# Moving part of the second layer's modulation products from the first layer's feed-forward into the second layer's mixer

## The chip, the cores and the metric

The kernel runs on one core of one Trainium2 chip. Its time is device microseconds of one execution; the median of several executions is compared. A profile of one execution shows what each engine did: TensorE (PE, with its weight loads as PEld), VectorE (DVE), ScalarE (ACT), GpSimd (POOL) and SyncE (SP), which issues every DMA here.

## The reference, cut to what matters

One inference step of a diffusion backbone: two layers over 640 tokens (128 of a prompt, 512 latent ones) of width 1024. Each layer is a mixer (four branches, gated and merged) and a convolutional feed-forward, both wrapped in modulated norms:

```python
def _trunk_layer(x, mod, lw, ctx):
    sh_a, sc_a, g_a, sh_f, sc_f, g_f = jnp.split(mod[:, None, :], 6, axis=-1)
    h = _rmsnorm(x, lw['g_pre_mix']) * (1.0 + sc_a) + sh_a
    m, cache = _token_mixer(h, lw, ctx)
    x = x + g_a * _rmsnorm(m, lw['g_post_mix'])
    h = _rmsnorm(x, lw['g_pre_ffn']) * (1.0 + sc_f) + sh_f
    x = x + g_f * _rmsnorm(_conv_ffn(h, lw), lw['g_post_ffn'])
    return x, cache
```

The modulation `mod` is `silu(cond) @ w_mod[i] + b_mod[i]`, 6144 numbers for each of two conditions (context and latent). They depend on no token, so they can be computed at any time before they are used. In blocks of 128 the 6144 are blocks 0 to 47: 0 to 15 are the shift and scale ahead of the mixer, 16 to 47 the gate, shift, scale and gate from the mixer's end on.

## The kernel before

Activations lie with features on the partitions, eight tiles of 128 x 640 for the width of 1024. Every linear layer streams its float32 weights in tiles of 128 x 512 (256 KB): a DMA brings `wr`, ScalarE rounds it to `wh`, VectorE takes the rest `wl = wr - wh`, and TensorE adds three products (`wh` with the activation's high part `ah`, `wh` with its low part `al`, `wl` with `ah`) in halves of 320 tokens.

The modulation products of everything but the first 16 blocks of layer 0 are not on TensorE. `mod_units` makes them on VectorE, one block of 128 outputs at a time, against a silu tile that is spread over all partitions:

```python
for j in blocks:
    for hf in hv:
        w = self.sbt(512, "wm", 2)
        self.load(w[:, :512], self.A["wmod"][l, j][:, hf * 512 : hf * 512 + 512])
        for q in range(2):
            ...
            self.nc.vector.scalar_tensor_tensor(junk[:, :512], w[:, :512], 0.5, si, ALU.mult, ALU.mult, accum_out=acc)
            yield
```

So a block is 2 loads of 256 KB into one of two buffers `wm` and 4 products ("units" from here on), each one VectorE instruction that writes `wj` and one that reads the accumulator. For each half `hv` the generator first loads the two conditions (`g<-in_c`), and ScalarE and VectorE make the silu tiles `silc`, two buffers.

The generator is drained in small portions. `fill(n)` takes n units from it and ties them to the TensorE instruction that was recorded last, so that they can't start before it. `merge` calls `fill(8)` ahead of each of 8 output blocks for the first and the third branch (64 units each; the second has `fill(0)`), `merge_out` calls `fill(2)` 16 times, the feed-forward calls `fill(5)` after each of its 22 up-projection blocks and `fill(2)` ahead of each block of a down-projection, and `fill(1000)` takes what is left.

In layer 0 the mixer's fills take 128 units, the blocks 16 to 47 of layer 0 itself. Then `mixer` starts a generator for all 48 blocks of layer 1: 192 units, of which 32 go in `merge_out` and 160 in the feed-forward of layer 0. In the mixer and the feed-forward of layer 1 nothing is left to fill with.

The program's order is not the order of the code. Every operation is recorded, then `order()` plays the whole kernel with a table of costs and emits it engine by engine in the order of the starts it found. A unit has the bias `BEHIND`, a late due time, unless what reads its result is due earlier; weight loads have the bias `AHEAD`. All instructions are issued from one line of the program (L608 in every row of the profile), so rows are told apart by their tiles. Each engine then works through its own list in order, SyncE with the DMA issues too.

Of the kernel before, what the change touches and what calls it, by code (L numbers as in the profile page):

```python
# [613 lines left out]
class Net:  # L614
# [1375 lines left out]
    def mixer(self, l, x, hh, hl):  # L1990

        nc, A = self.nc, self.A
        self.hb = self.sbt(32, "hb", 1)
        self.tsc(self.hb, self.P("bmg", 0, 32), 0.5)
        self.rope_load("64")
        win = A["win"][l]
        y = self.ssd(l, hh, hl)
        zd = self.spill("zd", 4)
        self.ph("ssd.z%d" % l)
        self.gates(win, range(W_Z, W_Z + 4), zd)(hh, hl)  # L2000
        r = self.ret_in(l, hh, hl)
        o = self.ssd_end(l, y, zd)
        r = self.ret_states(l, *r)
        gd = self.spill("gd", 4)
        self.ph("ret.g%d" % l)
        self.gates(win, range(W_RG, W_RG + 4), gd)(hh, hl)
        self.flush()
        merged = [self.X(j) for j in range(8)]
        o2 = self.ret(l, *r, gd)
        self.merge(l, 0, hh, hl, o, merged, 8)  # L2010
        self.flush()
        r = self.att_in(l, hh, hl)
        o = self.spill("od", 4)
        self.att(l, *r, o)
        self.merge(l, 1, hh, hl, o2, merged, 0)
        r = self.mla_in(l, hh, hl)
        o2 = self.spill("od", 4)
        self.mla(l, *r, o2)
        self.merge(l, 2, hh, hl, o, merged, 8)
        mods = self.modraw  # L2020
        if l == 0:
            self.fill(1000)
            self.mod_new()
            self.filler = self.mod_units(1, range(48), ((0,), (1,)), self.sil_tile)
        return self.merge_out(l, x, hh, hl, o2, merged, mods)

    def merge_out(self, l, x, hh, hl, o, merged, mods):
# [73 lines left out]
    def ffn(self, l, x, Gf, hh, hl):  # L2101
        A = self.A
        self.ph("ffn%d" % l)
        self.fcs = self.sbt(88, "fcs", 1)
        o, _ = PC["fcw"]
        for t in range(3):
            self.tsc(self.fcs[:, t * 22 : (t + 1) * 22], self.pc[:, o + t * 44 + 22 : o + t * 44 + 44], 0.5)
        o2, _ = PC["fcb"]
        self.tsc(self.fcs[:, 66:88], self.pc[:, o2 + 22 : o2 + 44], 0.5)
        acc = [self.O(j) for j in range(8)]  # L2110
        pre = [self.F() for _ in range(6)]
        specs = []
        for i in range(6):
            specs.append((A["wup"][l, (22 if i % 2 else 0) + i // 2], 8, hh, hl, 128,
                          lambda p, hv, i=i: self.conv_put(pre[i], p, hv)))
        self.lins(specs)
        fh, fl = {}, {}
        self.modw = self.g

        def up(f):  # L2120
            buf = pre[2 * f + 1] if f < 3 else self.conv_lin(A["wup"][l, 22 + f], 8, hh, hl)
            gt = self.conv(buf, [self.fcs[:, t * 22 + f : t * 22 + f + 1] for t in range(3)], self.fcs[:, 66 + f : 67 + f])
            sg = self.m()
            self.silu_half(sg[:, :641], gt[:, :641], 641)
            buf = pre[2 * f] if f < 3 else self.conv_lin(A["wup"][l, f], 8, hh, hl)
            up = self.conv(buf, [self.pc[:, o + t * 44 + f : o + t * 44 + f + 1] for t in range(3)], self.pc[:, o2 + f : o2 + f + 1])
            self.tt(sg[:, :641], sg[:, :641], up[:, :641])
            fh[f], fl[f] = self.F(F32R), self.F(F32R)
            for s, d in ((slice(0, 128), slice(0, 128)), (slice(129, 641), slice(128, 640))):
                self.act(fh[f][:, d], sg[:, s])  # L2130
                self.last = self.tt(fl[f][:, d], sg[:, s], fh[f][:, d], ALU.subtract)
            self.fill(5)

        def down(f0, f1):
            for j in range(8):
                self.fill(2)
                for p, c in self.lin_fm(A["wdn"][l, j][:, f0 * 128 : f1 * 128], f1 - f0, [fh[f] for f in range(f0, f1)], [fl[f] for f in range(f0, f1)]):
                    if f0 == 0:
                        self.act(acc[j][:, c], p)
                    else:  # L2140
                        self.last = self.tt(acc[j][:, c], acc[j][:, c], p, ALU.add)

        for f in FFN_ORDER:
            if isinstance(f, tuple):
                down(*f)
            else:
                up(f)
        f0, f1 = FFN_LAST
        self.fill(1000)
        Am = S = None  # L2150
        if l + 1 < L:
            self.params(l + 1)
            S, Am = self.mod_get(0, self.modraw), self.mod_scale(1, "gpm", self.modraw)
            hh, hl = self.split_tiles()
        fh, fl = [fh[f] for f in range(f0, f1)], [fl[f] for f in range(f0, f1)]
        norm = self.halves_to_norm(8, acc, acc, x, Gf, Am, S, hh, hl, "dn%d" % l, 1.0, self.xd[l + 1] if l + 1 < L else A["oy"])
        self.lins([(A["wdn"][l, j][:, f0 * 128 : f1 * 128], f1 - f0, fh, fl, 128, norm(j)) for j in range(8)])
        for k in range(8):
            self.dump("x", x[k][:, :T], l, k)
        return hh, hl  # L2160
# [38 lines left out]
```

## Time and profile before

| | us |
|---|---|
| median of 3 executions (lowest, highest) | 2915.98 (2914.49, 2923.48) |
| the profiled execution | 2915.53 |
| its span in the trace, first to last instruction | 2913.4 |
| TensorE busy | 2849.6 (98%) |
| VectorE busy | 2151.2 (74%) |
| ScalarE busy | 1390.3 (48%) |
| DMA queue of SyncE | 326.46 MB, 35.7% of 16 engines |

The span is 2.1 us shorter than the execution's own time. Shares are means over a span in which the stages differ much, so the two layers, which do the same work one after the other, are set side by side stage by stage.

### The profile page before, as it was taken

To read this page: it belongs to the slowest core of one execution; us is meant where nothing else is said; L and a number is where in the kernel's file an instruction comes from. 1 tells how busy PE (TensorE), PEld (TensorE's weight loads), DVE (VectorE), ACT (ScalarE), POOL (GpSimd) and SP (SyncE) were. 2 spreads that over 40 slices of the span, in tenths; PEclk is the share of its full clock that TensorE was granted. 3 is DMA by queue.
4 is the path that set the end of the run, shared out by engine and by line. 5 is a ranking of instruction groups with operands and counts; after the bars stand their busy time and mean duration, and the time that the engine had idled before them with its cause. 6 is when DMAs were issued, how large, how long until landed. Compare 5 with 4: busy or idle time off the path is not lost.

```text
span 2913.4 us, 50176 instructions
## 1 busy us (share of the span) xinstructions
PE 2849.6 (98%) x18638; PEld 2683.4 (92%) x18638; DVE 2151.2 (74%) x4548; ACT 1390.3 (48%) x3013; POOL 79.0 (3%) x99
## 2 busy tenths in 40 slices
PE   8999999999999999999989999999999999999998
PEld 4889998898899999999988899989988999999997
DVE  5895748648889899888878953586597577666667
ACT  4444347557735543333455443474576465333333
POOL 0000010000000000000000000100000000000000
PEclk9999999999999999999989999999999999999999
DMA  5224531234375444444332232212433444222223
GB/s 214 66 81 144 177 97 41 63 121 128 110 221 189 156 141 152 132 133 132 108 120 74 75 132 89 79 39 67 149 107 95 141 138 131 74 76 77 76 73 112
DMA packets 193412, 329.67 MB, mean 113 GB/s; under 512 B 20880, under 2 KB 54288, under 8 KB 193168
## 3 DMA queue, kind: packets, MB, share of 16 engines
q1 hardware_dynamic: 193168, 326.46, 35.7%
q8 instruction: 147, 2.41, 0.3%
q14 instruction: 97, 0.79, 0.1%
HBM read 293.41 MB, written 32.96 MB: 112 GB/s over the span
## 4 chain that ended last, share of the span: by engine, by line
PE 86%; DVE 6%; DMA 3%; issue 2%; ACT 1%; SPq 0%; POOL 0%; DVEq 0%; POOLq 0%; ACTq 0%
PE lin L608 70%; PE st L608 11%; PE pv L608 5%; DVE m L608 2%; DVE wl L608 1%; DMA wm<-in_wmod 1%; DVE wj L608 1%; DVE X L608 1%; DMA K<-in_wmod 0%; ACT K L608 0%; DVE al L608 0%; DMA vd<-g 0%; DVE K L608 0%; ACT m L608 0%; DVE g L608 0%
## 5 line engine op out<-in xcount | busy, mean ns | idle before, releaser
L608 PE MATMUL lin<-ah,wh 128*128 128x320 f32 (+1 forms) x3776 | 1158.3, 314 | 11.7 <-ACT K L608 6.9
L608 PE MATMUL lin<-al,wh 128*128 128x320 f32 (+1 forms) x3776 | 1150.4, 312 | 7.7 <-DVE al L608 7.5
L608 ACT ACTIVATE wh<-wr 128x512 fp32r<-128x512 f32 (+2 forms) x796 | 490.2, 617 | 1049.0 <-PE lin L608 725.7
L608 PE MATMUL lin<-ah,wl 128*128 128x320 f32 x3744 | 943.6, 311 | 0.5 <-DVE wl L608 0.4
L608 DVE TENSOR_TENSOR wl<-wr,wh 128x512 fp32r<-128x512 f32 (+2 forms) x790 | 530.0, 672 | 307.2 <-ACT wh L608 297.0
L608 PEld LDWEIGHTS lin<-ah,wh 128*128 128x128 f32 (+1 forms) x3776 | 710.2, 189 | 25.1 <-issue 8.8
L608 PEld LDWEIGHTS lin<-al,wh 128*128 128x128 f32 (+1 forms) x3776 | 708.1, 188 | 19.9 <-DVE al L608 11.4
L608 PEld LDWEIGHTS lin<-ah,wl 128*128 128x128 f32 x3744 | 649.2, 188 | 8.4 <-issue 3.8
L608 PE MATMUL lin<-K,wh 128*128 128x320 f32 (+1 forms) x1472 | 293.8, 313 | 6.1 <-DVE O L608 4.3
L608 DVE TENSOR_TENSOR m<-m,m 128x512 fp32r<-128x512 f32 (+6 forms) x393 | 246.3, 632 | 51.7 <-ACT m L608 45.5
L608 ACT ACTIVATE m<-st 128x512 fp32r<-128x512 f32 (+3 forms) x480 | 220.6, 524 | 102.7 <-PE st L608 90.0
L608 DVE SCALAR_TENSOR_TENSOR wj<-wm,silc 128x512 bf16<-128x512 f32 x320 | 219.8, 687 | 37.4 <-DMA wm<-in_wmod 34.2
L608 PEld LDWEIGHTS lin<-K,wh 128*128 128x128 f32 x1472 | 237.5, 189 | 8.5 <-ACT m L608 4.5
L608 PE MATMUL lin<-O,wh 128*128 128x320 f32 x1024 | 214.6, 311 | 0.4 <-DVE O L608 0.4
L608 PE MATMUL pv<-m,K 128*128 128x512 f32 (+2 forms) x832 | 204.6, 344 | 0.9 <-ACT m L608 0.5
L608 PE MATMUL lin<-K,wl 128*128 128x320 f32 (+1 forms) x736 | 185.0, 312 | 0.9 <-DVE wl L608 0.9
L608 PEld LDWEIGHTS lin<-O,wh 128*128 128x128 f32 x1024 | 166.9, 188 | 5.0 <-DVE O L608 0.7
L608 PEld LDWEIGHTS pv<-m,K 128*64 128x64 f32 (+1 forms) x832 | 116.2, 160 | 23.9 <-issue 6.2
L608 PE MATMUL st<-Q,K 128*128 128x512 f32 (+3 forms) x480 | 133.7, 381 | 0.1
L608 PE MATMUL lin<-O,wl 128*128 128x320 f32 x512 | 132.9, 310 | 0.0
L608 PEld LDWEIGHTS lin<-K,wl 128*128 128x128 f32 x736 | 128.4, 189 | 1.6 <-DVE wl L608 1.6
L608 DVE TENSOR_REDUCE nm<-st 128x1 f32<-128x320 f32 (+1 forms) x288 | 122.7, 461 | 7.3 <-PE st L608 5.8
(195 smaller groups left out, 2957.2 us busy)
## 6 DMA issues: line engine op xcount, KB each, us to landing
wr<-in_wup SPq DMA_DIRECT2D x196, 256.0 KB, 2.7
wr<-in_wmg SPq DMA_DIRECT2D x160, 256.0 KB, 2.8
wm<-in_wmod SPq DMA_DIRECT2D x160, 256.0 KB, 3.0
wr<-in_win SPq DMA_DIRECT2D x142, 256.0 KB, 2.6
wr<-in_wdn SPq DMA_DIRECT2D x94, 256.0 KB, 2.7
wr<-in_wbr SPq DMA_DIRECT2D x80, 256.0 KB, 2.7
wr<-in_wout SPq DMA_DIRECT2D x64, 256.0 KB, 2.8
g<-od SPq DMA_DIRECT2D x32, 320.0 KB, 4.1
```

The source lines that it names most:

```text
L608: f(*[_plain(v) for v in o.args], **{k: _plain(v) for k, v in o.kw.items()})
```

## The change

The generator of layer 1 is split. Blocks 0 to 15 (64 units) stay where all 48 were: 32 units in `merge_out` of layer 0 and 32 in its feed-forward, now three after each up-projection block in place of five. Blocks 16 to 47 (128 units) get a generator of their own, which is set up at the end of layer 0's feed-forward and is drained by the fills that layer 1's mixer has already, `fill(8)` ahead of each output block of its first and third merge. The `fill(1000)` in `mixer` is now called in both layers.

```diff
         mods = self.modraw
+        self.fill(1000)
         if l == 0:
-            self.fill(1000)
             self.mod_new()
-            self.filler = self.mod_units(1, range(48), ((0,), (1,)), self.sil_tile)
+            self.filler = self.mod_units(1, range(16), ((0,), (1,)), self.sil_tile)
         return self.merge_out(l, x, hh, hl, o2, merged, mods)
...
                 self.last = self.tt(fl[f][:, d], sg[:, s], fh[f][:, d], ALU.subtract)
-            self.fill(5)
+            self.fill(3)
...
             S, Am = self.mod_get(0, self.modraw), self.mod_scale(1, "gpm", self.modraw)
             hh, hl = self.split_tiles()
+            self.filler = self.mod_units(l + 1, range(16, 48), ((0,), (1,)), self.sil_tile)
```

## Rows read from the trace of the kernel before

**Rows 1.** The page: busy time by engine, and the chain that ended last.
```profile
PE 2849.6 (98%) x18638; PEld 2683.4 (92%) x18638; DVE 2151.2 (74%) x4548; ACT 1390.3 (48%) x3013; POOL 79.0 (3%) x99
PE 86%; DVE 6%; DMA 3%; issue 2%; ACT 1%; SPq 0%; POOL 0%; DVEq 0%; POOLq 0%; ACTq 0%
```

**Rows 2.** Everything on tile `wm`: durations in ns min/median/max, first and last start.
```profile
L608 DVE SCALAR_TENSOR_TENSOR wj<-wm,silc x320: 672/685/696, 278.2 to 1390.5; 128x512 bf16<-128x512 f32 x160
L608 DVE DVE_READ_ACCUMULATOR wj<-wm,silc x320: 73/82/86, 278.8 to 1391.2; 128x1 f32 x160
L608 SPq DMA_DIRECT2D wm<-in_wmod x160: 327/328/1765, 271.1 to 1382.6; - x160
DMA to landing us min/median/max: 2.4/3.0/6.2
```

**Rows 3.** Long pieces of the whole chain: start, length, what, matmuls.
```profile
1052.28 366.03 PE lin L608 x2494
...
2486.08 366.05 PE lin L608 x2494
```

**Rows 4.** Equal stretches of both layers: length, busy times, PEclk, DMA share, GB/s.
```profile
260.15:386.47 126.32, 122.88 (x876) 120.82 (x874) 90.52 (x235) 42.01 (x110) 8.66 (x14) 1.00 0.56 174
1709.56:1831.95 122.39, 122.39 (x876) 120.82 (x874) 47.73 (x105) 40.11 (x108) 8.03 (x14) 1.00 0.34 104
795.08:916.78 121.70, 116.82 (x774) 114.65 (x772) 110.24 (x268) 54.23 (x103) 0.00 (x0) 0.99 0.70 217
2237.38:2350.06 112.68, 112.68 (x772) 112.68 (x770) 63.20 (x102) 52.54 (x99) 0.00 (x0) 1.00 0.44 135
916.78:996.30 79.52, 78.42 (x535) 76.99 (x535) 72.20 (x181) 47.63 (x100) 3.13 (x3) 1.00 0.54 170
2350.06:2430.08 80.02, 78.21 (x536) 77.27 (x537) 60.90 (x141) 47.55 (x100) 3.74 (x3) 1.00 0.45 139
1052.28:1418.31 366.03, 366.03 (x2496) 366.03 (x2497) 323.63 (x736) 126.54 (x286) 0.00 (x0) 1.00 0.43 132
2486.08:2852.13 366.05, 366.05 (x2496) 366.05 (x2497) 232.93 (x408) 123.50 (x284) 0.00 (x0) 1.00 0.25 75
```

**Rows 5.** The same stretches, VectorE's instructions on `wj` alone (two a unit).
```profile
260.15:386.47 126.32, 44.58 (x128) 1.00 0.56 174
...
795.08:916.78 121.70, 52.76 (x152) 0.99 0.70 217
...
916.78:996.30 79.52, 13.94 (x40) 1.00 0.54 170
...
1052.28:1418.31 366.03, 110.87 (x320) 1.00 0.43 132
```

**Rows 6.** TensorE's waits, first merge of layer 0: total us, times, longest.
```profile
PE st L608 <- DVE m L608: 3.4, 2, 2.3
```

**Rows 7.** TensorE's waits from the third merge to the first output half, layer 0.
```profile
PE lin L608 <- DVE al L608: 3.9, 3, 2.0
```

**Rows 8.** VectorE's waits in that stretch.
```profile
DVE wj L608 <- DMA wm<-in_wmod: 9.3, 13, 1.6
```

**Rows 9.** SyncE's waits ahead of a DMA issue in that stretch.
```profile
SPq L608 <- DVE wj L608: 28.4, 35, 1.8
```

**Rows 10.** The chain in that stretch: start, length, what.
```profile
864.31 0.70 DVE wj L608 x2
865.03 4.50 DMA wm<-in_wmod
...
892.29 0.41 DVE al L608
892.75 24.03 PE lin L608 x162
```

**Rows 11.** GpSimd's powers in the first merge, layer 0.
```profile
L608 POOL TENSOR_TENSOR rq<-rq,mhalf 128x4 f32<-128x4 f32 x5 | 5.7, 1138 | 64.1 <-DVE rq L608 64.1
```

**Rows 12.** The same in the first merge of layer 1.
```profile
L608 POOL TENSOR_TENSOR rq<-rq,mhalf 128x4 f32<-128x4 f32 x5 | 5.0, 1008 | 59.1 <-DVE rq L608 59.1
```

**Rows 13.** A pair of stretches with no unit in either layer.
```profile
618.57:795.08 176.51, 171.16 (x1036) 150.23 (x1035) 139.53 (x247) 126.81 (x270) 5.18 (x13) 1.00 0.40 128
2064.07:2237.38 173.31, 171.50 (x1036) 150.22 (x1035) 139.63 (x247) 127.08 (x270) 5.18 (x13) 1.00 0.40 127
```

## The prediction

> **What bounds the kernel now.** Start with the page: TensorE is busy for 98% of the span, VectorE for 74%, and the chain that ended last is 86% TensorE [rows 1]. So time is lost only where something makes TensorE stop, and a gain can come only from such a place. The mean does not say where the units hurt. For that the kernel carries its own control: both layers run the same mixer and the same feed-forward, layer 0 with units in its gaps and layer 1 without any. The whole chain gives pieces of TensorE work that recur in both layers with the same count; taken as boundaries, they give equal stretches whose lengths can be subtracted.
>
> First look at the feed-forward, which the change relieves. It is one unbroken piece of 2494 matmuls in each layer, 366.03 us with units and 366.05 us without [rows 3]. In the table of stretches TensorE is busy for the whole of both, although VectorE works 323.63 us in one and 232.93 us in the other [rows 4]. VectorE at 88% still never makes TensorE wait there.
>
> Then look at the mixer, which the change loads. From the first merge on, 876 matmuls take 126.32 us in layer 0, where 64 units run, and 122.39 us in layer 1: 3.93 us more. From the third merge to the norm after the first half of the output projection it is 121.70 us against 112.68 us: 9.02 us more, with TensorE never idle in layer 1. The stretch after that is 0.50 us shorter in layer 0 (79.52 against 80.02) although it holds 20 units [rows 4, 5].
>
> What the reader is to see in the waits: TensorE waits for `m` of VectorE in the first merge (3.4 us in two waits, 2.3 the longest) [rows 6] and for `al`, the low half of the activations, in the later stretch (3.9 us in three) [rows 7]. Behind both is VectorE's in-order list. There it waits for `wm` to land (9.3 us in 13 waits) [rows 8], and SyncE in turn waits 28.4 us for VectorE to give a `wm` buffer back [rows 9], with weight loads behind it in the same queue. The chain shows the loop: two products, a `wm` transfer of 4.50 us, later `al`, then TensorE [rows 10].
>
> **The change part by part.** *The count.* 48 blocks are 192 units, 16 are 64, the other 32 are 128. The merges of layer 1 call for 8 x 8 units twice, 128, so the new generator is used up in the mixer and both `fill(1000)` find at most its end. Layer 0's mixer and `merge_out` keep the units they have: the first 32 of the old and of the new generator are the same blocks and the same half. In layer 0's feed-forward 160 units become 32.
>
> *What is taken out.* 128 units leave the feed-forward of layer 0. Each is a product of 685 ns and an accumulator read of 82 ns, 0.767 us, so 98.2 us of VectorE; with them go 64 loads of 256 KB, 328 ns each on SyncE, 21.0 us of its list [rows 2]. All lay beside 366.03 us of gapless TensorE [rows 3, 4]. Gain: 0. The cover would have to be gone for it to be worth more, and the layer without any unit shows that it then takes 366.05 us. The last product ended near 1391 us [rows 2], before the stretch ends, so the norm that follows does not wait for units either. `fill(3)` only spaces the 32 units that remain; 0, for the same reason.
>
> *What is added.* The new generator loads the two conditions and makes silu tiles for each half, four sets more than before: 4 loads of 256 KB, 4 ScalarE passes and 4 VectorE passes of the units' shape, by their row some 0.69 us each. In layer 0's stretches the same sets lie inside the difference already, so they are not added again.
>
> *What is put in: the first merge of layer 1.* 64 units with 32 loads, the same instructions at the same fills as layer 0 has. Bound from below: 0, if the waits in layer 0 were chance. From above: the whole 3.93 us. VectorE's work goes from 47.73 to about 97 us of 122 (64 x 0.767 = 49.1), which is not full, yet layer 0 with 90.52 us lost 3.93 [rows 4]. I take 3.93, since it is the same code under the same load.
>
> A small share of this may come over GpSimd. Five powers on the way to the retention norm take 1138 ns each in layer 0 [rows 11] and 1008 ns in layer 1 [rows 12], 0.65 us in all. The Trainium skill, "SBUF — State Buffer", section "Who interferes with whom", has a VectorE instruction with two inputs in SBUF contend with a GpSimd instruction that reads SBUF, and a unit reads two. The rows agree in sign; by that rule alone the added time of this merge would be about 0.65 us, an estimate, against the 3.93 us of the stretches.
>
> *What is put in: the third merge of layer 1.* 64 units, 32 loads, and a new wait: `merge_out` needs gate, shift and scale from these units for the norm after the first output half. Before, they were ready long ahead. Queued behind a late unit on VectorE are `wl` of the weights, `al` of the activations and the gates' products, and TensorE waits for each of them. Price from below: 0. From above: 9.02 us. VectorE's need is 63.20 + 49.1 = 112.3 us in a stretch of 112.68 us, with waits for `wm` on top (9.3 us in layer 0), so it can't all fit. One thing is different: layer 0's stretch holds 76 units, 12 of them of the next set [rows 5]. These come last, when the 24.03 us piece of TensorE from 892.75 on is running already [rows 10], so I do not count them as a cause. I take 9.02.
>
> *What follows it.* The stretch after gave 0.50 us back in layer 0, which I take as the end of the same shift: -0.50. The norm was not late there, so I price the new wait itself at 0. The granted clock was 0.99 to 1.00 in all these stretches [rows 4], so I add nothing for it.
>
> Sum: 0 + 3.93 + 9.02 - 0.50 = 12.45 us, on the profiled execution's 2915.53: 2927.98, say 2928. The median of the runs is 2915.98, half a microsecond from that execution, so the sum holds for the median as well.
>
> **The rivals.** *Hidden (not slower).* The place is VectorE's list between layer 1's third merge and the first output half, and what decides is whether its 112.3 us of work run with under a microsecond of waits, or 9 us of units slide into later gaps. For it: VectorE is at 56% there (63.20 of 112.68), and TensorE's own waits in layer 0 are just 3.4 and 3.9 us, with some transfers of 4.50 us against a median of 3.0 [rows 2, 10], which may be chance. Against: the units are due at the norm, so they can't slide far, and at 0.70 the DMA share in that stretch is high [rows 4]. It gives 2915.5. The Trainium skill, "Perfetto Trace Analysis", section "Optimization Strategy", has it that regimes with different most-contended engines may be interleaved to gain; by that rule, work taken from an engine share of 88% to one of 56% should do no harm. The trace does not bear it out, as far as layer 0 goes.
>
> *One stall only.* The plan for layer 1 meets one of the two places at better moments. Then 3.93 or 8.52 remain: 2919.5 to 2924.1.
>
> *More than a copy of layer 0.* The shift also disturbs stages without units. How large that can be, a pair of stretches without any shows: the same 1036 matmuls took 176.51 us in one layer and 173.31 us in the other, 3.20 us apart [rows 13]. On top of 12.45 that gives 2931.2, and should the norm be late as well by as much, 2934.4.
>
> *Faster.* Relief in layer 0's feed-forward lets TensorE reach the next layer sooner. It needs idle time there, and there is none to take [rows 4]; only a reordering of the emitted lists elsewhere could give some, at most the same 3.20 us were the losses hidden too: 2912.3, and over 0.3% it would need more than any row offers.
>
> **How the numbers follow.** A change of 0.3%, about 8.7 us, is about what a measurement of this kernel can tell from no change. Copy of layer 0 (2925 to 2931): 0.60. One stall only: 0.18. Hidden: 0.12. More than a copy: 0.06. Faster than 2915: 0.04. The time is that of the first, 2928. For the range I go from 2917, inside the gap between hidden and one stall, to 2934; that leaves out the hidden case and the faster one, and a little at the top, under 2 in 10. Slower by over 0.3% means above 2924.7: the copy, more than a copy, and the upper end of one stall, 0.69. Within 0.3%: hidden, most of one stall and most of faster, 0.28. Faster by over 0.3%: 0.03.
>
> **What would show it.** The feed-forward of layer 0 still one piece of 366.0 us, with VectorE near 250 us (232.93 and 32 units of 0.767) in place of 323.63. Layer 1's first merge stretch near 126.3 us and its third near 121.7 us, with waits of TensorE for `m` and `al`, and waits of VectorE for `wm`, in layer 1 too. Layer 0's own stretches as they were. Wrong would be: layer 1's stretches at 122.4 and 112.7 us with the units in them (hidden), the norm after the first output half late, or layer 0's feed-forward under 366 us.

## The result, and the profile after

The changed kernel took 2938.70 us, median of 4 executions (2930.36 to 2940.08), beside 2917.64 us for the kernel before: a ratio of 1.006, 95% interval 1.0045 to 1.0075. Run a second time among the experiments it took 2941.02 us against 2919.16, a ratio of 1.0078 (1.0063 to 1.0093). So the change makes the kernel some 18 to 23 us slower by the ratios; the medians lie 21.06 and 21.86 us apart. The direction and two of the three places that lose were forecast; the time lies above the forecast range, whose top was 2934.

The page of the changed kernel's profiled execution (2938.97 us, span 2937.0 us), against [rows 1]:

```profile
PE 2859.5 (97%) x18638; PEld 2688.8 (92%) x18638; DVE 2163.7 (74%) x4552; ACT 1390.3 (47%) x3017; POOL 79.7 (3%) x99
PE 85%; DVE 7%; DMA 4%; issue 3%; ACT 1%; SPq 0%; POOL 0%; DVEq 0%; POOLq 0%; ACTq 0%
```

The same matmuls, 10 us more of TensorE time for them, and a share of the chain that went from TensorE to VectorE, DMA and issue. Where, the long pieces of the chain say (start, length, matmuls), against [rows 3]:

```profile
1020.08 35.33 PE lin L608 x236
1057.91 367.57 PE lin L608 x2494
...
2509.33 366.04 PE lin L608 x2494
```

Layer 0's feed-forward did not gain, as forecast, but it lost: 367.57 us in place of 366.03. Ahead of it stands a place that the prediction did not look at. The table of stretches, same columns as [rows 4], shows the four that the change touches: start and rest of layer 0's feed-forward, then the first and the third merge of layer 1.

```profile
1020.08:1057.91 37.83, 35.76 (x239) 34.98 (x239) 36.88 (x72) 21.97 (x46) 0.00 (x0) 1.00 0.41 133
1057.91:1425.48 367.57, 367.57 (x2496) 367.57 (x2497) 251.84 (x471) 122.47 (x281) 0.00 (x0) 1.00 0.27 84
1716.53:1844.36 127.83, 124.65 (x875) 122.66 (x874) 90.55 (x235) 41.33 (x110) 8.68 (x14) 0.99 0.55 169
2250.07:2373.33 123.26, 117.53 (x772) 114.41 (x770) 103.54 (x243) 53.07 (x101) 0.00 (x0) 0.99 0.63 196
```

The kernel before needed 36.02 us for the first of them in either layer:

```profile
1016.26:1052.28 36.02, 35.75 (x239) 34.97 (x239) 35.07 (x67) 19.64 (x41) 0.00 (x0) 1.00 0.38 122
2450.06:2486.08 36.02, 35.75 (x238) 34.96 (x239) 34.93 (x66) 19.63 (x41) 0.00 (x0) 1.00 0.34 108
```

So in this execution the start of the feed-forward costs 1.81 us (37.83 - 36.02), its rest 1.54 (367.57 - 366.03), the first merge 5.44 (127.83 - 122.39) and the third 10.58 (123.26 - 112.68), 19.37 us together. The executions differ by 23.44 us (2938.97 - 2915.53); the other 4.07 us lie in stretches that the change does not touch, 1.81 of them in layer 0's own first merge. In the second profiled execution the same four stretches were 37.87, 367.53, 128.17 and 123.98 us, 20.43 us together, against 22.8 us by its ratio.

In the merges the waits are those of layer 0, where the kernel before has none in layer 1. TensorE's waits in layer 1's first merge (total us, times, longest), to be read against [rows 6], and the three largest in its third, against [rows 7]:

```profile
PE st L608 <- DVE m L608: 3.2, 2, 2.9
```
```profile
PE lin L608 <- DVE al L608: 3.0, 3, 2.1
PE lin L608 <- DVE wl L608: 1.0, 2, 0.6
PE lin L608 <- ACT O L608: 0.9, 1, 0.9
```

and what it waits for in the third, as the chain has it there (start, length, what):

```profile
2285.20 3.48 DMA wm<-in_wmod
...
2291.42 0.75 DVE O L608
2292.17 0.02 issue
2292.19 3.50 DMA g<-od
2295.68 0.02 issue
2295.71 0.75 ACT O L608
2296.45 0.02 issue
2296.47 0.84 DVE O L608
2297.31 0.04 issue
2297.36 38.94 PE lin L608 x253
```

The reader is to see the loop that layer 0 had: a load of `wm`, products on VectorE, a late operation that TensorE needs, here the third merge's own input `O`, whose load `g<-od` stands in the same SyncE queue.

At the start of layer 0's feed-forward it is something else. The one wait of TensorE that grew there, in the kernel before and in the changed one (total us, times, longest):

```profile
PE lin L608 <- DVE Q L608: 0.3, 1, 0.3
```
```profile
PE lin L608 <- DVE Q L608: 2.1, 1, 2.1
```

The timeline of VectorE, and then of TensorE, in the changed kernel (start, length, engine, operation, and in brackets the idle time before it and who ended it):

```profile
1054.13 1.28 DVE L608 SCALAR_TENSOR_TENSOR silc<-silc,g 128x512 f32<-128x512 f32 x2
1055.34 1.69 DVE L608 TENSOR_TENSOR K<-m,K 128x128 fp32r<-128x128 f32 x4
1056.94 0.68 DVE L608 TENSOR_TENSOR wl<-wr,wh 128x512 fp32r<-128x512 f32 x1
1057.55 0.35 DVE L608 TENSOR_SCALAR Q<-lin 128x2 f32<-128x2 f32 x4
```
```profile
1055.38 0.46 PE L608 MATMUL lin<-ah,wl 128*128 128x320 f32 x2
1057.91 0.39 PE L608 MATMUL lin<-ah,wh 128*128 128x320 f32 x1 [2.07 <-DVE Q L608]
...
1058.47 0.47 PE L608 MATMUL lin<-al,wh 128*128 128x320 f32 x1
```

Two passes that make silu tiles take 1.28 us in a row of VectorE work without a gap, ahead of the `Q` that ends TensorE's wait, and TensorE stands for 2.07 us. Then its matmuls take 0.47 us each in place of 0.31. That is the clock: the table gives the granted share in four short stretches of this execution.

```profile
1014.00:1017.40 3.40, 3.40 (x15) 3.40 (x15) 0.16 (x1) 0.00 (x0) 0.85 (x1) 0.50 0.19 71
1058.40:1061.70 3.30, 3.30 (x15) 3.30 (x14) 3.30 (x7) 0.00 (x0) 0.00 (x0) 0.50 0.29 84
1775.20:1778.50 3.30, 2.79 (x12) 2.82 (x13) 2.89 (x9) 0.00 (x0) 0.00 (x0) 0.50 0.60 156
2297.40:2300.80 3.40, 3.40 (x13) 3.40 (x14) 3.34 (x9) 0.63 (x1) 0.00 (x0) 0.50 0.51 171
```

0.50 is 1.2 GHz of 2.4; such a stretch at the lower clock is called a spell below. Three of the four stand at a wait of TensorE that grew with the change (2.07 us) or is new with it (2.9 and 0.9 us in the merges). The rest of the feed-forward, which has no wait of its own, shows the price of a spell: 1.54 us.

### The profile page after: what moved, and what is told of

Its sections match the earlier page's. It is cut to its first block, busy times and chain, and to the rows that moved or that the text cites. A ratio compares the mean times of both kernels' runs of the same rounds, so it can differ in the third digit from the quotient of the medians.

```text
span 2937.0 us, 50190 instructions
## 1 busy us (share of the span) xinstructions
PE 2859.5 (97%) x18638; PEld 2688.8 (92%) x18638; DVE 2163.7 (74%) x4552; ACT 1390.3 (47%) x3017; POOL 79.7 (3%) x99
## 4 chain that ended last, share of the span: by engine, by line
PE 85%; DVE 7%; DMA 4%; issue 3%; ACT 1%; SPq 0%; POOL 0%; DVEq 0%; POOLq 0%; ACTq 0%
PE lin L608 69%; PE st L608 10%; PE pv L608 5%; DVE m L608 2%; DVE wl L608 1%; DMA wm<-in_wmod 1%; DVE wj L608 1%; DVE X L608 1%; DMA vd<-g 1%; DVE g L608 0%; ACT m L608 0%; DMA g<-in_c 0%; SPq L608 0%; DMA m<-in_cak 0%; DVE al L608 0%
## 5 line engine op out<-in xcount | busy, mean ns | idle before, releaser
L608 POOL TENSOR_TENSOR rq<-rq,mhalf 128x3 f32<-128x3 f32 (+3 forms) x41 | 58.1, 1418 | 2583.0 <-DVE rq L608 2583.0
```

The source lines that it names most:

```text
L608: f(*[_plain(v) for v in o.args], **{k: _plain(v) for k, v in o.kw.items()})
```

## The experiments

All were timed in five rounds beside the kernel before. The last four columns are lengths in us of the stretches of the table above, found in each trace by the same matmuls; the kernel before has 36.02, 366.03, 122.39 and 112.68. Edits are shown against the changed kernel where the text does not say otherwise; unchanged code between them is left out.

| kernel | ratio to before (95% interval) | start of feed-forward | rest of it | first merge, layer 1 | third merge, layer 1 |
|---|---|---|---|---|---|
| changed kernel, again | 1.0078 (1.0063 to 1.0093) | 37.87 | 367.53 | 128.17 | 123.98 |
| late fill | 1.0052 (1.0033 to 1.0070) | 36.03 | 366.03 | 128.84 | 121.37 |
| silu tiles late | 1.0053 (1.0037 to 1.0070) | 36.05 | 366.03 | 128.12 | 121.40 |
| first merge only | 1.0017 (1.0005 to 1.0029) | 36.02 | 366.03 | 128.88 | 112.67 |
| third merge only | 1.0035 (1.0021 to 1.0049) | 36.05 | 366.03 | 122.40 | 125.19 |
| short products | 1.0049 (1.0031 to 1.0067) | 37.84 | 367.57 | 126.57 | 118.26 |
| no loads | 1.0025 (1.0015 to 1.0036) | 37.82 | 366.03 | 122.44 | 116.58 |
| both short | 1.0023 (1.0011 to 1.0034) | 37.83 | 366.03 | 122.46 | 115.44 |
| spread, on the changed kernel | 1.0000 (0.9987 to 1.0013) | 37.85 | 366.02 | 122.50 | 115.20 |
| spread and silu tiles late, on the changed kernel | 0.9983 (0.9972 to 0.9995) | 36.02 | 366.03 | 122.79 | 114.84 |

**The changed kernel again.**

> The changed kernel itself again, beside the experiments on one chip, since executions of one kernel differ by up to 20 us here. Both theories: 15 to 22 us over the kernel before; the same lists, so the same places lose: the start of layer 0's feed-forward some 3.4 us, the first merge of layer 1 4 to 6 us, the third 9 to 11 us, and spells at the lower clock that come and go between executions.

Measured: ratio 1.0078, 22.8 us at 2919.16, a little above what was expected; the places as expected, the third merge (11.30 us) a little above too. Every engine's list stands in the same order as in the first trace, so what differs is the execution. Of its stretches, the two merges:

```profile
1713.59:1841.76 128.17, 124.01 (x875) 122.19 (x874) 90.45 (x235) 41.95 (x110) 8.68 (x14) 0.99 0.56 169
2247.27:2371.25 123.98, 117.27 (x772) 114.14 (x770) 103.57 (x243) 53.14 (x101) 0.00 (x0) 0.99 0.62 194
```

**Late fill: is the start of the feed-forward a cost of the change?**

```diff
-            self.fill(3)
+            self.fill(3 if f > 4 else 0)
```

> The changed kernel, but layer 0's feed-forward draws no units until its up-projection block 5, so the silu tiles of the second half are made in the middle of the feed-forward and not at its dense start. Theory A (the start of the feed-forward is a third place where the change costs, 4.9 us in the trace after: silu tiles ahead of wl and the last rounding on VectorE, then a spell at the lower clock): that stretch returns to 56 us and the kernel is 3 to 5 us faster than the changed one, some 17 us slower than the kernel before. Rival B (those 4.9 us are drift of one profiled execution, only the merges of layer 1 count): no change against the changed kernel, some 21 us slower than before.

The stretch returned to 36.03 us and the one behind it to 366.03:

```profile
1022.11:1058.14 36.03, 35.75 (x239) 34.98 (x239) 34.94 (x66) 19.65 (x41) 0.00 (x0) 1.00 0.34 108
```

The ratio fell to 1.0052. The stretches bear theory A out; the timing alone does not, since the intervals (1.0033 to 1.0070 here, 1.0045 to 1.0075 and 1.0063 to 1.0093 for the changed kernel) overlap. Of the 4.9 us named in the expectation, some 1.5 are the granted clock's spell at 1014 us, which this run has too, at the same place (0.50 from 1016.2 to 1019.5 us), and so has the kernel of the first merge only, whose start of the feed-forward loses nothing; so it is not that wait's.

**Silu tiles late: the plan's urgency.**

```diff
         for hv in halves:
             sil = {}
+            self.rec.bias = BEHIND
```

> The changed kernel, but the loads and passes that make silu tiles get the same late due time as the units themselves; nothing else moves. Theory A (they cost because the plan takes them as urgent work): the start of layer 0's feed-forward is 3 to 5 us shorter, and each merge with units 0 to 1 us shorter, so 3 to 7 us faster than the changed kernel. Rival B (the units themselves, not the silu tiles, are what hurts): within 1 us of the changed kernel, about 21 us over the kernel before.

The start of the feed-forward was 36.05 us, as with the late fill; the first merge stayed at 128.12 us. The third was 121.40 us with the clock at 1.00, so it lost 8.72 us here without a spell; the late fill, with layer 1's lists unchanged, lost 8.69 us with one:

```profile
2238.89:2360.29 121.40, 115.95 (x772) 112.84 (x770) 103.12 (x243) 53.20 (x101) 0.00 (x0) 1.00 0.65 199
```

So theory A held for the start of the feed-forward alone. In the merges rival B held: there the units hurt, not the silu passes. Ratio 1.0053.

**First merge only, third merge only: a price per place or per unit.** Layer 0 keeps blocks 0 to 31 of layer 1, and layer 1's mixer gets 32 to 47:

```diff
-            self.filler = self.mod_units(1, range(16), ((0,), (1,)), self.sil_tile)
+            self.filler = self.mod_units(1, range(32), ((0,), (1,)), self.sil_tile)
...
-            self.fill(3)
+            self.fill(5)
...
-            self.filler = self.mod_units(l + 1, range(16, 48), ((0,), (1,)), self.sil_tile)
+            self.filler = self.mod_units(l + 1, range(32, 48), ((0,), (1,)), self.sil_tile)
```

The second of the two also has

```diff
-        self.merge(l, 0, hh, hl, o, merged, 8)
+        self.merge(l, 0, hh, hl, o, merged, 0 if l else 8)
```

> Only 64 units move to layer 1's mixer, all of them into its first merge; the other 128 stay in layer 0's merge_out and feed-forward with fill(5). Theory A (a price per place): 4 to 5.5 us over the kernel before, the stretch of the first merge near 127 us and that of the third at 112.7 us. Rival C (a price per unit, wherever it runs in the mixer): half of the whole, some 8 to 10 us.

> Only 64 units move to layer 1's mixer, all of them into its third merge; the other 128 stay in layer 0 with fill(5). Theory A (a price per place): 9 to 11 us over the kernel before, the stretch of the third merge near 122 to 123 us, that of the first at 122.4 us. Rival C (a price per unit): some 8 us, as much as with the first merge alone.

Each changed its own stretch and left the other as it was. The first merge only:

```profile
1717.98:1846.86 128.88, 124.66 (x876) 122.60 (x874) 92.19 (x243) 43.18 (x112) 8.68 (x14) 0.99 0.57 172
2251.90:2364.57 112.67, 112.67 (x771) 112.67 (x770) 63.20 (x102) 52.56 (x99) 0.00 (x0) 1.00 0.44 135
```

Ratios 1.0017 and 1.0035, 5.0 and 10.2 us of the 2920.55 us that the kernel before took beside them: the third merge takes twice the price for the same 64 units, so the price is the place's. Each alone lost a little more than in the changed kernel, 6.49 and 12.51 us, and more than was expected (near 127 us, and 122 to 123 us). Its 64 units are then 32 of either half, so the silu tiles of both halves are made in one place; that this is the reason is not shown. Layer 0's feed-forward stayed at 366.03 us with 64 units more than in the changed kernel.

**Short products, no loads, both short: what it is in a merge that hurts.** In layer 1's mixer alone, a product over 64 of 512 columns with the plan's cost held; then whole products with one load a half; then load and product both of 64 columns with both costs held. The edits of the first two are shown, without the line that holds the plan's cost. In the traces of short products and of both short every engine's list has the order of the changed kernel.

```diff
-                            self.nc.vector.scalar_tensor_tensor(junk[:, :512], w[:, :512], 0.5, si, ALU.mult, ALU.mult, accum_out=acc)
+                            n_ = 64 if l and blocks[0] == 16 else 512
+                            self.nc.vector.scalar_tensor_tensor(junk[:, :n_], w[:, :n_], 0.5, si[:, :n_], ALU.mult, ALU.mult, accum_out=acc)
```
```diff
-                    w = self.sbt(512, "wm", 2)
-                    self.load(w[:, :512], self.A["wmod"][l, j][:, hf * 512 : hf * 512 + 512])
+                    if not (l and blocks[0] == 16) or j == 16:
+                        w = self.sbt(512, "wm", 2)
+                        self.load(w[:, :512], self.A["wmod"][l, j][:, hf * 512 : hf * 512 + 512])
```

> The changed kernel, but each of the 128 units in layer 1's mixer multiplies 64 of its 512 columns (the rest of the sum is left out); its loads stay whole, and the plan keeps the old cost for it, so that the order of every engine's list is the same. Theory D (VectorE's time is what makes TensorE wait in the merges): the third merge's stretch falls from 123 to 113 to 115 us, the first's to 123 or 124, some 12 to 14 us less than the changed kernel. Rival Q (the transfers of wm and the SyncE queue behind them are what hurts): 0 to 4 us less.

> The changed kernel, but in layer 1's mixer only the first block's weights of each half are loaded and all 32 blocks of the half are multiplied with them: 62 of 64 wm loads are left out there, the products are whole. Theory D (VectorE's time): 9 us or more of the loss in the two merges stays, since VectorE needs 112.3 us of 112.7 us in the third. Rival Q (transfers and queue): the stretches return to 122.4 and 112.7 us, 12 to 16 us less than the changed kernel.

> The changed kernel, but each of the 128 units in layer 1's mixer loads and multiplies 64 of its 512 columns (the rest of the sum is left out), while the plan keeps the old costs of both, so that every engine's list stands in the same order. It completes a table of four: whole, short products, no loads, both short. Theory P (products and loads are each a part of the price): first merge's stretch 122.4 to 123 us, third's 113 to 115 us, so 11 to 16 us less than the changed kernel; what stays is the start of layer 0's feed-forward. Rival O (the order of the lists itself, with TensorE work put where a late activation was planned, is the price): 4 us or more of the third merge's loss stays.

Short products, the two merges, and the product's own row in the first merge (count, busy, mean ns, idle before):

```profile
1714.58:1841.15 126.57, 124.14 (x876) 122.34 (x874) 61.61 (x235) 41.38 (x110) 8.33 (x14) 0.99 0.55 171
2246.72:2364.98 118.26, 115.85 (x772) 114.32 (x770) 76.13 (x243) 53.14 (x101) 0.00 (x0) 0.99 0.65 204
```
```profile
L608 DVE SCALAR_TENSOR_TENSOR wj<-wm,silc 128x64 bf16<-128x64 f32 x64 | 14.2, 223 | 16.0 <-DMA wm<-in_wmod 14.5
```

No loads:

```profile
1717.71:1840.15 122.44, 122.44 (x876) 120.87 (x874) 89.82 (x235) 41.29 (x110) 9.39 (x14) 1.00 0.36 110
2245.12:2361.70 116.58, 114.29 (x772) 112.75 (x770) 103.94 (x243) 53.41 (x101) 0.00 (x0) 1.00 0.44 137
```

Both short, third merge:

```profile
2235.94:2351.38 115.44, 114.28 (x772) 112.75 (x770) 75.89 (x243) 53.35 (x101) 0.00 (x0) 1.00 0.49 146
```

The two merges answer differently. In the first, VectorE's time is free: 89.82 us of it without loads cost 0.05 us, while 61.61 us of it with the loads cost 4.18. A product of 223 ns then only waits longer for its weights (14.5 us). The cleanest pair is short products and both short, the same lists with the loads whole or of 64 columns: 126.57 and 122.46 us. Rival Q, the transfers and the queue behind them, is right there.

In the third merge both count: of 8.7 to 11.3 us, short products leave 5.58 (with a spell in it, the clock is at 0.99) and missing loads 3.90. With both short 2.76 us remain, at a granted clock of 1.00. That is more than theory P allowed and less than rival O asked for; it is the part that shorter units don't give back, and whether it is the order itself or the short units that still run is open. The no-load kernel is the weaker witness, as it has another order in layer 1: the plan saw the missing loads. For the whole kernel neither D nor Q had its figure: short products are 8.5 us below the changed kernel by the ratios, between the two.

**Spread: too much in two places?** Units as 5, 6, 5 over the three merges, on the kernel before (layer 0 alone) and on the changed one (both layers), and as 4, 8, 4 on the kernel before, and with the silu tiles late on the changed one. The first of these edits, against the kernel before:

```diff
-        self.merge(l, 0, hh, hl, o, merged, 8)
+        self.merge(l, 0, hh, hl, o, merged, 5)
...
-        self.merge(l, 1, hh, hl, o2, merged, 0)
+        self.merge(l, 1, hh, hl, o2, merged, 6)
...
-        self.merge(l, 2, hh, hl, o, merged, 8)
+        self.merge(l, 2, hh, hl, o, merged, 5)
```

> The kernel before, with layer 0's own 128 units spread over three merges (fill 5, 6, 5 in place of 8, 0, 8); layer 1 has none. If a price per place that is too full on VectorE is what counts (D), layer 0's 12.9 us shrink to less than half and this is 5 to 10 us faster than the kernel before. If each unit in a mixer costs some 0.1 us wherever it runs (C), no change within 2 us.

> The changed kernel with the mixers' 128 units spread over three merges in both layers (fill 5, 6, 5 in place of 8, 0, 8). Theory P (the price is that of too much in two places): both layers lose 3 to 5 us each, so the kernel is 18 to 24 us faster than the changed one and within 8 us of the kernel before. Rival C (moving units into any mixer costs): 10 us or more over the kernel before.

> The kernel before with layer 0's own 128 units as 4, 8, 4 over the three merges; layer 1 has none. Theory P: the second merge, among the attention heads, still has room on VectorE (149 us of 232 us busy), so this is 11 to 14 us faster than the kernel before, the same as 5, 6, 5 or a little better. If 8 there is too much for that place, it is worse than 5, 6, 5 by some us.

> The changed kernel with 4, 8, 4 units in the merges of both layers and the late due time for the loads and passes that make silu tiles. Theory P: the start of layer 0's feed-forward loses nothing, the merges 1 to 4 us per layer: 4 us faster to 4 us slower than the kernel before. Rival C: 8 us or more slower than the kernel before.

On the kernel before, 5, 6, 5 gave 2906.99 us against 2919.16, ratio 0.9962 (0.9951 to 0.9974), and 4, 8, 4 gave 2908.66 against 2919.07, ratio 0.9964 (0.9953 to 0.9975): the same within their intervals, and both faster than the kernel before and the changed one. The first is a little more than was expected, the second a little less. Layer 0's first and third merge with 5, 6, 5, against 126.32 and 121.70 us in [rows 4], and the long stretch between, in which the second merge lies:

```profile
260.54:384.24 123.70, 122.61 (x876) 120.81 (x874) 75.00 (x187) 42.02 (x110) 8.36 (x14) 1.00 0.48 153
791.90:908.28 116.38, 114.26 (x773) 113.02 (x773) 98.45 (x224) 53.65 (x101) 0.00 (x0) 1.00 0.63 200
384.24:616.34 232.10, 232.05 (x1475) 211.76 (x1474) 179.94 (x363) 130.53 (x273) 14.60 (x8) 1.00 0.28 89
```

The kernel before has this for the last of them:

```profile
386.47:618.57 232.10, 232.05 (x1474) 211.75 (x1474) 149.26 (x269) 129.23 (x271) 14.62 (x8) 1.00 0.19 60
```

The 48 units in it cost nothing: 232.10 us, TensorE busy for 232.05, with and without them. On the changed kernel the same spread brings the ratio to 1.0000 (0.9987 to 1.0013), some 20 us below the changed kernel, and with the silu tiles late and 4, 8, 4 to 0.9983 (0.9972 to 0.9995), 5 us below the kernel before, where 4 were expected at best. Rival C, which asked for 10 us and 8 us or more over the kernel before, is out.

That does not make the move free. With the same spread on both sides it still costs: 1.0000 against 0.9962, some 11 us, for 5, 6, 5, and 0.9983 against 0.9964, some 5 us with intervals that just touch, for 4, 8, 4. In the traces of 5, 6, 5 the columns of the table show 1.83 us of it at the start of the feed-forward, 0.11 in layer 1's first merge and 2.52 in its third. The mean granted clock of the twelve executions was 0.9906 with the move and 0.9928 without; by estimate that is some 6 us of 2915, and why it was lower there is open. Layer 1's third merge is 115.20 us with 5, 6, 5 and 114.84 with 4, 8, 4, in place of 112.68:

```profile
2234.56:2349.76 115.20, 113.37 (x772) 112.77 (x770) 88.18 (x190) 52.47 (x99) 0.00 (x0) 1.00 0.56 177
```

## Why the prediction was wrong

That the two merges of layer 1 would lose as layer 0's do, and that the feed-forward would gain nothing, was right. Four terms were not: the units left in the feed-forward (put at 0, measured 3.35 us), the first merge (3.93, measured 5.44 and 5.78), the third (9.02, measured 10.58 and 11.30) and what follows it (-0.50, measured 0). The first is a mechanism that was missing, the others are sizes.

*"What is taken out ... Gain: 0"* was right: layer 0's feed-forward takes 366.03 us with 32 units (where no spell of the clock falls into it), with 96 and with 160, and 366.05 in layer 1 with none. (The 250 us of VectorE that it named there is a slip: 232.93 and 32 units of 0.767 are 257.5; 251.84 were measured.)

*"`fill(3)` only spaces the 32 units that remain; 0"* is a step that failed. Splitting the generator also moves the point where the second half starts. With 16 blocks it comes after 32 units, at the first draw of the feed-forward, in place of well inside it; there the silu tiles are made, and the passes that make them have no late due time. They stood ahead of `wl` and the last rounding in a gapless list of VectorE: 1.80 to 1.85 us, and in three of six traces a spell of the clock behind it, 1.5 us. Late fill and silu tiles late each took the wait away. The prediction counted the silu tiles that are added, but did not ask where the ones that stayed would now stand. In both profiled executions of the changed kernel this term, put at 0, was 3.35 us.

*"The granted clock was 0.99 to 1.00 ... so I add nothing for it"* failed too. The 0.99 in layer 0's third merge was a spell, and 9.02 us contained it; the first merge's 3.93, at 1.00, did not:

```profile
881.20:884.50 3.30, 3.30 (x14) 3.30 (x14) 3.27 (x11) 0.00 (x0) 0.00 (x0) 0.50 0.77 225
```

In layer 1 the first merge had one in each trace where it lost more than half a microsecond (0.99).

*The copy of layer 0* was the right mechanism with terms too small: 3.93 became 5.44 and 5.78, 9.02 became 10.58 and 11.30 in the two profiled executions of the changed kernel. Both prices had been read from one execution. In the ten traces with 8, 0, 8 units in layer 0, the first merge there took from 126.3 us, in the kernel before, which is the lowest of the ten, to 130.2. In the changed kernel's trace, without a spell, and in that of the first merge only, with one:

```profile
261.26:389.38 128.12, 123.56 (x875) 121.31 (x874) 90.48 (x235) 41.74 (x110) 8.67 (x14) 1.00 0.55 169
260.34:390.51 130.17, 125.36 (x876) 122.88 (x874) 90.68 (x235) 42.03 (x110) 8.66 (x14) 0.99 0.55 170
```

So layer 1's 127.83 and 128.17 us lie where layer 0's own do, and 3.93 was a low draw. Layer 0's third merge took 120.7 to 122.8 us in the same ten, 8.0 to 10.2 us over layer 1's without units; layer 1's 10.58 and 11.30 lie above that. The same lists of layer 1 lost 8.69 us in the late fill, so a part of it is the execution too; the rest is open.

*"The norm was not late"* held: the stretch behind the third merge was 80.02 us in the changed kernel (2373.33 to 2453.35), as long as in layer 1 before, so the 0.50 us that I took off was not given back. Together these terms make 19.37 and 20.43 us where 12.45 stood.

*VectorE's time as the bound in the third merge* (112.3 of 112.68 us) was a part of the truth: with short products 5.58 us stayed, without loads 3.90, and 2.76 with both short. In the first merge the transfers and SyncE's queue were what counted. The 3.93 us from the stretches were nearer than the share of GpSimd: without loads its powers were slower still, 1282 ns each, and the first merge lost 0.05 us; with both short they took 1009 ns. So the rule of the Trainium skill, "SBUF — State Buffer", section "Who interferes with whom", agrees with the durations, and is worth nothing in the time here.

*Hidden* and *one stall only* are refuted by the stretches. *More than a copy* came nearest in time, 2931.2 to 2934.4, but not by what it named: the stretches of layer 1 without units stayed as they were within 0.2 us, and the norm was not late. The rule of the Trainium skill, "Perfetto Trace Analysis", section "Optimization Strategy", that interleaving regimes may gain, did not come true for two merges with 64 units each; it did for the stretch of layer 0's second merge, which took 48 units for nothing.

## What to carry to other kernels

A second layer that does the same work without the moved part is a good price list for it, but a price read from one trace is one draw: look at the same stretch in several, and read the clock's column with it, since a stretch at 0.99 holds a spell and one at 1.00 may get one. When a generator of background work is split, look for what it does at each start, not only for what it yields. Background work is limited by the fullest place it is put in, in transfers and queue as much as in engine time; spreading it won back what the move had cost, but on the kernel before it won some 11 us as well, so there it was worth having without the move.

## What the runs showed of the hardware

A wait of TensorE of 2.07 us was followed by a spell at 1.2 GHz of some 3.4 us, worth 1.54 us, in a stretch that otherwise is 366.02 or 366.03 us in every trace of the table. Such spells come and go: the same wait stands in six traces, and a spell followed it in the changed kernel's two and with short products, not with no loads, both short, or the spread without late silu tiles.

Much of the difference between executions lies in a stretch that no kernel here changes, from the end of layer 0's feed-forward to layer 1's first merge: 263.14 us at a granted clock of 0.97 with silu tiles late, 266.60 at 0.95 in the kernel before, and 271.65 at 0.93 in the spread on the changed kernel.

The kernel before, 24 times beside the first experiments, took from 2910.03 to 2929.96 us, so that effects of 5 us needed many rounds, or a trace.

A third buffer for `wm` was not tried.
